# One core's diffusion backbone step: where the sums for the fast FFN product are formed, which first pairs leave the second 512 tokens out, and which engine does the norm's affine maps

## The chip, the cores and the metric

One core of a Trainium2 chip runs the whole inference step in one launch. The metric is device time in microseconds; the kernel before takes 3452.81 us, the median of 3 runs from 3447.42 to 3453.67. TensorE (PE) multiplies matrices out of SBUF into PSUM banks, VectorE (DVE), ScalarE (ACT) and GpSimd (POOL) do the elementwise work, and SyncE (SP) issues most DMAs; ScalarE and GpSimd issue some too. Each engine takes its instructions in the order in which they are written.

## The reference

Two layers, each a token mixer (S5 in layer 0, grouped-query attention in layer 1) and a SwiGLU FFN, on 1024 latent and 256 context tokens of width 1024. Cut to what the change touches:

```python
z = jax.nn.gelu(y)                               # S5 mixer
val, gate = jnp.split(z @ w_glu, 2, axis=-1)
ms = (val * jax.nn.sigmoid(gate)) @ w_out
xs = layer_norm(ALPHA * xs + g1 * ms, ln_g, ln_b)  # x for the residual
h = xs * (1.0 + sc2) + sh2                         # modulate
gate, up = jnp.split(h @ w_in, 2, axis=-1)         # FFN, w_in 1024 x 5632
fs = (jax.nn.silu(gate) * up) @ w_out              # 2816 x 1024
xs = layer_norm(ALPHA * xs + g2 * fs, ln_g, ln_b)
```

## The kernel before, in words

Activations lie transposed: 128 channels (a tile `kt` of 8) by tokens, in three chunks: c=0 and c=1 are 512 latent tokens each, c=2 the 256 context tokens. All matrix products run in float32 through a split: an operand x becomes hi = x rounded to TensorE's fast float32 form (ScalarE, a copy) and lo = x - hi (a subtract), and a product is hi*hi + hi*lo + lo*hi, three matmuls.

**The fast product.** `Ffn` computes the GLU of the S5 layer (8 pairs) and the first product of both FFNs (22 pairs each). A pair is 128 columns of gate and the 128 of up that belong to them. Over its latent tokens a pair is a product of 2x2 blocks (gate/up by chunk c=0/c=1 and by halves of the channels), done by a Strassen-Winograd scheme with 7 products instead of 8; each is 12 matmuls of 128x512 (L946). The weight side needs A11, A12, A21, A22 and the sums S1 to S4 (`i_step`), made anew for each pair. The token side needs B11, B21 (the two halves of c=0), B22 (second half of c=1) and the sums T1 to T4 of c=0 and c=1 (`x_next`: a subtract L848 on VectorE, hi L851 on ScalarE, lo L852 on VectorE or GpSimd by turns; 4 tiles each); they are made once per matrix. The context goes separately, as G and U, 24 matmuls of 128x256 each (L956). A whole pair is `FULL`: P1 P5 P6 P2 P7 G P4 P3 U.

P1 and P2 need only c=0 and G, U only the context. So the first pairs (`GF` = 2 in the GLU, `FF1` = 3 in each FFN) are cut in two: first all the `HEAD`s (P1, P2, G, U), before c=1 is ready, then the `TAIL`s (P6, P5, P7, Z3, P4). P1's product stays in its PSUM bank from head to tail, and the tail's P6, P7, P4 accumulate onto it; Z3 has a bank of its own. The first tail's steps call `x_all` for the sums they need (`ready` in `ffn_body`), so that T1, T2 are written ahead of P6, T3 ahead of P5, B22 ahead of P7, T4 ahead of Z3.

**The boundaries.** Between the output product of one sublayer and the first product of the next stands a layer norm over channels. `boundary` interleaves the output product, the norms' steps (a generator per chunk, `layer_norm`) and the heads, by an estimated clock and the estimated costs that each step yields. A norm of a chunk is: mean by a ones matmul (L695), subtract and square, the sum of squares (L711), rsqrt on VectorE (13 small instructions), its spread to all partitions (L691), then per tile a multiply (L718) and an affine map to h (even tiles on ScalarE L730, odd on VectorE L728). After these come 8 second affine maps in place to the residual (even on ScalarE L752, odd on GpSimd L748), each followed by a DMA of the tile to DRAM from the same engine's queue (`keep`, L1521). Last, h is split (`h_split`, hi L825, lo L826). Such boundaries stand before FFN 0, before the attention, before FFN 1, and, with no h, at the end.

Weights come by SyncE's DMAs, two raw half pages per pair; `AHEAD` = 4 operands are split ahead of their use. Pages (88 of 128x512) and half pages (13) are pools that wait for the last reader.

Of the kernel before, what the change touches and what calls it, by code (L numbers as in the profile page):

```python
# [613 lines left out]
class Dense(S5):  # L614
# [64 lines left out]
    def layer_norm(self, acc, c, cols, raw, ready, after=None):  # L679
# [36 lines left out]
        for kt in range(KT):  # L716
            a = acc[kt][c]
            v.tensor_tensor(a, a, pr, op=ALU.mult)  # L718
            if A is not None:
                if c < 2:  # L720
                    t = self.page()
                elif kt % 2 == 0:
                    pair = self.page(F32, (P, 2, 256))
                if c == 2:
                    t = pair[:, kt % 2, :]
                raw[kt][c] = t
                if kt % 2:
                    v.tensor_scalar(t, a, A[:, kt, cd:cd + 1], B[:, kt, cd:cd + 1], op0=ALU.mult, op1=ALU.add)  # L728
                else:
                    nc.scalar.activation(t, a, AF.Identity, bias=B[:, kt, cd:cd + 1], scale=A[:, kt, cd:cd + 1])  # L730
            else:
                self.affine(acc, cols, kt, c, after)
            if kt % 2:
                yield YW[5] * n / 512
        ready[c] = True
        if A is not None:
            for kt in range(KT):
                self.affine(acc, cols, kt, c, after)
                if kt % 2:
                    yield YW[6] * n / 512  # L740

    def affine(self, acc, cols, kt, c, after):
# [4 lines left out]
        if kt % 2 if cols[0] is not None else c == 2 and kt in (1, 3, 5):  # L747
# [8 lines left out]
    def boundary(self, outs, passes, ln, heads, ready):  # L756
# [41 lines left out]
        "P6": ("S2", "T2"), "P7": ("S3", "T3"), "Z3": ("S4", "B22")}  # L798
# [4 lines left out]
TAIL = ("S1", "S2", "S3", "S4", "A22"), ("P6", "P5", "P7", "Z3", "P4")  # L803

AHEAD = 4
# [4 lines left out]
class Ffn(Dense):  # L810
# [18 lines left out]
    def x_next(self, n):  # L829

        nc, r = self.nc, self.xr
        v, g = nc.vector, nc.gpsimd
# [4 lines left out]
        eng = (v, g)[k % 2]  # L837
        if n == "C":
            self.h_split(k, 2, eng)
        elif n[0] == "B":  # L840
            kt, c = k + 4 * (n[1] == "2"), int(n[2]) - 1
            self.h_split(kt, c, eng)
            self.X[n][k] = self.hs[kt, c]
        else:
# [7 lines left out]
            eng.tensor_tensor(lo, t, hi.bitcast(F32), op=ALU.subtract)  # L852
# [7 lines left out]


    def i_start(self, win, pairs, first):
# [3 lines left out]
        self.segs = [(t, HEAD) for t in p[:first]] + [(t, TAIL) for t in p[:first]] + [(t, FULL) for t in p[first:]]  # L866
# [4 lines left out]
    def i_load(self):  # L871
        if self.il < len(self.segs):
            r = []
            for h in range(2):
# [6 lines left out]
    def i_step(self):  # L881
# [6 lines left out]
        if a < n:  # L888
# [3 lines left out]
            g, u = self.iraw[i]  # L892
# [32 lines left out]
    def ffn_step(self, i, kind, act):  # L925
# [33 lines left out]
        if kind == "P1":  # L959
            R = product("R", True)  # L960
            e["s1"] = self.page()
            ac(e["s1"], R, AF.Copy)
        elif kind == "P2":
            B = product("B", True)
            v.tensor_tensor(e["s1"], e["s1"], B, op=ALU.add)  # L965
            ac(e["s1"], e["s1"], act)
        elif kind == "P5":
            product("Q", True)
        elif kind == "P6":
            R = product("R", False)  # L970
            e["s2"] = self.page()
            ac(e["s2"], R, AF.Copy)
        elif kind == "P7":
            R = product("R", False)
            x = e["t22"] = self.page()
            v.tensor_copy(x, e["Q"])
            v.tensor_tensor(x, x, R, op=ALU.add)
        elif kind == "P4":
            R = product("R", False)
            v.tensor_tensor(e["s1"], e["s1"], R, op=ALU.mult)  # L980
            self.spill(t, 0, e["s1"])
        elif kind in ("P3", "Z3"):
# [18 lines left out]
    def ffn_heads(self, act, first):  # L1001

        U = []
        for i in range(first):
            for kind in HEAD[1]:
                U.append((kind, lambda i=i, kind=kind: self.ffn_step(i, kind, act)))
        h0 = [lambda: self.x_all("B11", "B21")] + [u for k, u in U[:2]]
        h2 = [lambda: self.x_all("C")] + [u for k, u in U[2:]]
        return [(0, h0), (2, h2)]

    def ffn_body(self, act, first, last):
        ready = {0: ("T1", "T2"), 1: ("T3",), 2: ("B22",), 3: ("T4",)}
        for i in range(first, len(self.segs)):
# [462 lines left out]
NHP = 13, 88  # L1476

GF, FF1 = 2, 3


class Full(Attn):
# [31 lines left out]
    def rest(self):  # L1513
# [58 lines left out]
        self.ffn_body(AF.Sigmoid, GF, last)  # L1572
        acc = new()
# [5 lines left out]
        def ffn(l, cols, outs, acc, passes):  # L1579

            raw = self.xr
            self.cross(outs, TWO, acc, cols, raw, ready, self.ffn_heads(AF.Silu, FF1), keep)
# [431 lines left out]
```

## Time and profile before

| what | before |
|---|---|
| median of 3 runs | 3452.81 us |
| the profiled execution | 3445.47 us, its span 3443.4 us |
| mean granted TensorE clock | 0.957 |
| TensorE busy | 3200.7 us, 93% |
| VectorE busy | 2126.4 us, 62% |
| ScalarE busy | 1350.6 us, 39% |
| GpSimd busy | 402.4 us, 12% |
| L946 (the fast products) | 1053.7 us busy, 81.4 us idle before it |
| L956 (the context) | 323.2 us busy, 21.4 us idle before it |

Busy time is the sum of an engine's instructions in one execution; the idle time before a line is how long the engine stood still ahead of that line's instructions, with what ended it. The span starts at 0 for all times below. TensorE is busy almost throughout, so time is lost only where it waits or runs at a lower granted clock.

### The profile page before, as it was taken

The numbers are of one execution on the slowest core, as the hardware profiler recorded it, in microseconds if no ns is written. First come the engines' busy times: TensorE is split into PE (matmuls) and PEld (weight loads), VectorE is DVE, ScalarE is ACT, GpSimd is POOL, SyncE is SP. The second block draws the span as 40 slices with busy tenths as digits, with TensorE's granted clock in tenths as the row PEclk, the third lists the DMA queues.
The fourth block names the chain that finished last, engine by engine and source line by source line (L and its number), as shares of the span: only waits on it lengthen the run. The fifth ranks groups of instructions, "written<-read, shape, count | busy, mean of one in ns | idle before, by whom it ended". The sixth has DMA issues, their size and how long they took to land.

```text
span 3443.4 us, 46852 instructions
## 1 busy us (share of the span) xinstructions
PE 3200.7 (93%) x17674; PEld 2678.0 (78%) x17674; DVE 2126.4 (62%) x4317; ACT 1350.6 (39%) x2667; POOL 402.4 (12%) x420
## 2 busy tenths in 40 slices
PE   8999669997799999999989999999779999999997
PEld 5753647886588888887878899998558888888776
DVE  8789745557754444524676888885775444453645
ACT  3351432335422222412443577774442222232433
POOL 2230120013200000010232310001230000000001
PEclk9999779998899999999999999999879999999998
DMA  7679952243222221624421100102322121244544
GB/s 262 168 215 324 253 137 76 87 157 114 83 71 68 65 75 61 207 65 140 143 93 57 62 21 16 35 1 94 112 87 78 60 80 60 80 152 137 170 128 137
DMA packets 226563, 381.42 MB, mean 111 GB/s; under 512 B 54608, under 2 KB 109680, under 8 KB 225568
## 3 DMA queue, kind: packets, MB, share of 16 engines
q1 hardware_dynamic: 208000, 332.49, 30.7%
q0 software_dynamic: 10128, 33.22, 3.0%
q10 hardware_dynamic: 8208, 12.72, 1.0%
q8 instruction: 138, 2.26, 0.3%
q14 instruction: 89, 0.73, 0.1%
HBM read 297.61 MB, written 80.74 MB: 110 GB/s over the span
## 4 chain that ended last, share of the span: by engine, by line
PE 76%; DVE 12%; issue 4%; ACT 3%; DMA 3%; SPq 1%; POOL 1%; ACTq 0%; DVEq 0%; POOLq 0%
PE ps L946 27%; PE ps L123 9%; PE ps L121 9%; PE ps L125 9%; PE ps L956 8%; PE ps L1375 2%; DVE sw L537 1%; PE ps L1396 1%; PE ps L1395 1%; PE ps L1394 1%; PE ps L1333 1%; PE ps L1334 1%; PE ps L1335 1%; DVE X L543 1%; DVE sw L541 1%
## 5 line engine op out<-in xcount | busy, mean ns | idle before, releaser
L946 PE MATMUL ps<-pg,pg 128*128 128x512 f32 x4368 | 1053.7, 399 | 81.4 <-ACT pg L851 43.7
L946 PEld LDWEIGHTS ps<-pg,pg 128*128 128x128 f32 x4368 | 830.8, 193 | 273.6 <-ACT pg L851 50.9
L121 PE MATMUL ps<-pg,pg 128*128 128x512 f32 (+1 forms) x1872 | 639.7, 364 | 33.8 <-ACT pg L131 18.9
L123 PE MATMUL ps<-pg,pg 128*128 128x512 f32 (+1 forms) x1872 | 634.0, 361 | 5.7 <-DVE pg L132 3.7
L125 PE MATMUL ps<-pg,pg 128*128 128x512 f32 (+1 forms) x1872 | 629.1, 358 | 0.2 <-DVE pg L103 0.2
L121 PEld LDWEIGHTS ps<-pg,pg 128*128 128x128 f32 x1872 | 349.9, 191 | 98.6 <-ACT pg L131 23.3
L123 PEld LDWEIGHTS ps<-pg,pg 128*128 128x128 f32 x1872 | 349.7, 191 | 65.1 <-DVE pg L132 9.2
L125 PEld LDWEIGHTS ps<-pg,pg 128*128 128x128 f32 x1872 | 349.5, 191 | 52.8 <-DVE pg L103 1.3
L956 PE MATMUL ps<-pg,pg 128*128 128x256 f32 x2496 | 323.2, 287 | 21.4 <-ACT pg L825 21.4
L956 PEld LDWEIGHTS ps<-pg,pg 128*128 128x128 f32 x2496 | 319.6, 196 | 30.0 <-ACT pg L825 22.4
L102 ACT ACTIVATE pg<-wr 128x512 fp32r<-128x512 f32 x344 | 192.0, 597 | 362.7 <-DMA wr<-in_w_ffn_out 168.0
L103 DVE TENSOR_TENSOR pg<-wr,pg 128x512 fp32r<-128x512 f32 x344 | 261.2, 798 | 102.8 <-ACT pg L102 91.3
L631 DVE SCALAR_TENSOR_TENSOR pg<-ps,mods,pg 128x512 f32<-128x512 f32 x64 | 47.9, 749 | 275.4 <-PE ps L125 266.2
L910 DVE TENSOR_TENSOR pg<-pg,pg 128x512 fp32r<-128x512 f32 x208 | 143.0, 687 | 77.4 <-ACT pg L906 77.4
L1105 POOL TENSOR_TENSOR pg<-pg,pg 128x512 f32<-128x512 f32 x8 | 10.7, 1332 | 1523.4 <-DVE pg L631 968.6
L132 DVE TENSOR_TENSOR pg<-ps,pg 128x512 fp32r<-128x512 f32 (+1 forms) x210 | 141.8, 676 | 58.9 <-ACT pg L131 53.3
L910 DVE TENSOR_TENSOR pg<-wr,pg 128x512 fp32r<-128x512 f32 x216 | 154.5, 719 | 24.4 <-ACT pg L906 24.4
L1355 ACT ACTIVATE pg<-ps,nb,rq 128x512 f32<-128x512 f32 x192 | 148.8, 776 | 5.6 <-DVE sm L1364 2.6
L131 ACT ACTIVATE pg<-ps 128x512 fp32r<-128x512 f32 (+1 forms) x210 | 123.3, 588 | 67.8 <-PE ps L1375 47.6
L980 DVE TENSOR_TENSOR pg<-pg,ps 128x512 f32<-128x512 f32 x52 | 35.7, 687 | 178.1 <-PE ps L946 177.9
L965 DVE TENSOR_TENSOR pg<-pg,ps 128x512 f32<-128x512 f32 x52 | 35.7, 687 | 175.1 <-PE ps L946 174.4
L906 ACT ACTIVATE pg<-wr 128x512 fp32r<-128x512 f32 x216 | 132.1, 620 | 14.6 <-DMA wr<-in_w_s_glu 12.9
(341 smaller groups left out, 4738.1 us busy)
## 6 DMA issues: line engine op xcount, KB each, us to landing
wr<-in_w_ffn_in SPq DMA_DIRECT2D x100, 512.0 KB, 3.6
gw<-in_w_mod SPq DMA_DIRECT2D x192, 256.0 KB, 5.0
wr<-in_w_ffn_out SPq DMA_DIRECT2D x80, 512.0 KB, 3.8
dI<-pg SPq DMA_DIRECT2D x104, 256.0 KB, 4.6
pg<-dI SPq DMA_DIRECT2D x104, 256.0 KB, 4.9
wr<-in_w_ffn_out SPq DMA_DIRECT2D x40, 384.0 KB, 3.9
pg<-dX SPq DMA_DIRECT2D x48, 256.0 KB, 4.0
wr<-in_w_s_glu SPq DMA_DIRECT2D x20, 512.0 KB, 3.7
```

What stands on the lines that cost most here:

```text
L102: nc.scalar.activation(hi, x, AF.Copy)
L103: nc.vector.tensor_tensor(lo, x, hi.bitcast(F32), op=ALU.subtract)
L121: mm(ps[c], wh, rh[c], start=first, stop=False)
L123: mm(ps[c], wh, rl[c], start=False, stop=False)
L125: mm(ps[c], wl, rh[c], start=False, stop=last)
L131: self.nc.scalar.activation(hi, src, AF.Copy)
L132: self.nc.vector.tensor_tensor(lo, src, hi.bitcast(F32), op=ALU.subtract)
L906: nc.scalar.activation(hi, self.isum[i, name], AF.Copy)
L910: v.tensor_tensor(lo, self.isum[i, name], hi.bitcast(F32), op=ALU.subtract)
L946: mm(e[bank], p[:, o], q, start=(first and k == 0 and j == 0), stop=(k == 3 and j == 2), skip_group_check=True)
L956: mm(ps, p[:, o], q, start=(k == 0 and j == 0), stop=(k == KT - 1 and j == 2))
L1355: nc.scalar.activation(p, u["bank"].pop((qt, kc)), AF.Exp, bias=nb[:, 0:1], scale=rq, accum_out=sm[:, kc:kc + 1])
```

## The change

- `layer_norm`: all 8 affine maps to h on ScalarE; `affine`: all 8 second maps and their DMAs on ScalarE's queue (the final norm is as before).
- `x_next`: all lo subtracts on VectorE.
- `x_rest` yields T1, T2, T3, T4, B22 one tile at a time; the norm of c=1 takes two of them behind each of its 8 second affine maps, the rest behind the last. In the GLU two are taken behind each product from the third on.
- `GF` = (5, 0), `FF1` = (2, 3): 5 pairs are cut in two everywhere. The first 5 (GLU) or 2 (FFN) of them have `HEAD0` (P1, P2, one raw half page) and `TAIL0` (P6 P5 P7 G P4 P3 U), the other 3 of an FFN `HEAD` and `TAIL`.
- P1's product is copied to a page at once; in a tail P6 starts a fresh bank, VectorE adds the page to it (L992 of the changed kernel), P7 goes on in the same bank, and the page is added again for P7 and P4. P3 accumulates onto P5 and P7's bank, so Z3 is gone.
- `AHEAD` = 3 in heads and tails and 5 after; the norm's costs count 1.4 times (`YS`) in the FFN boundaries; 12 half pages; c=1 of the GLU's input is loaded before the context.

```diff
@@ layer_norm, affine
-                if kt % 2:
-                    v.tensor_scalar(t, a, A[:, kt, cd:cd + 1], B[:, kt, cd:cd + 1], op0=ALU.mult, op1=ALU.add)
-                else:
-                    nc.scalar.activation(t, a, AF.Identity, bias=B[:, kt, cd:cd + 1], scale=A[:, kt, cd:cd + 1])
+                nc.scalar.activation(t, a, AF.Identity, bias=B[:, kt, cd:cd + 1], scale=A[:, kt, cd:cd + 1])
...
         if A is not None:
+            then = iter(then)
             for kt in range(KT):
                 self.affine(acc, cols, kt, c, after)
-                if kt % 2:
-                    yield YW[6] * n / 512
+                t = next(then, 0.0) + next(then, 0.0)
+                if kt % 2 or t:
+                    yield t or YW[6] * n / 512
+            yield from then
...
-        if kt % 2 if cols[0] is not None else c == 2 and kt in (1, 3, 5):
+        if cols[0] is None and c == 2 and kt in (1, 3, 5):
@@ order of the first pairs
-TAIL = ("S1", "S2", "S3", "S4", "A22"), ("P6", "P5", "P7", "Z3", "P4")
-
-AHEAD = 4
+TAIL = ("S1", "S2", "S3", "A22", "S4"), ("P6", "P5", "P7", "P4", "P3")
+
+HEAD0 = ("A11", "A12"), ("P1", "P2")
+TAIL0 = ("S1", "S2", "S3", "A11", "A12", "A22", "S4", "A21"), ("P6", "P5", "P7", "G", "P4", "P3", "U")
+
+AHEAD = 3, 5
+
+YT, YS = 1.8, 1.4
@@ x_next
-            eng.tensor_tensor(lo, t, hi.bitcast(F32), op=ALU.subtract)
+            v.tensor_tensor(lo, t, hi.bitcast(F32), op=ALU.subtract)
...
+    def x_rest(self, *names):
+
+        for n in names or ("T1", "T2", "T3", "T4", "B22"):
+            while self.x_next(n):
+                yield YT
@@ ffn_step
+        self.x_all(*{"T2": ("T1", "T2"), "T4": ("T1", "T2", "T4")}.get(PROD.get(kind, (0, "C"))[1], (PROD.get(kind, (0, "C"))[1],)))
...
         elif kind == "P6":
-            R = product("R", False)
+
+            R = product("R", tail)
+            if tail:
+                e["p1"] = e["s2"]
             e["s2"] = self.page()
-            ac(e["s2"], R, AF.Copy)
+            if tail:
+                v.tensor_tensor(e["s2"], e["p1"], R, op=ALU.add)
+            else:
+                ac(e["s2"], R, AF.Copy)
         elif kind == "P7":
             R = product("R", False)
             x = e["t22"] = self.page()
-            v.tensor_copy(x, e["Q"])
+            if tail:
+                v.tensor_tensor(x, e["p1"], e["Q"], op=ALU.add)
+            else:
+                v.tensor_copy(x, e["Q"])
             v.tensor_tensor(x, x, R, op=ALU.add)
@@ constants and the GLU
-NHP = 13, 88
-
-GF, FF1 = 2, 3
+NHP = 12, 88
+
+GF, FF1 = (5, 0), (2, 3)
...
-        for c in (0, 2, 1):
+        for c in (0, 1, 2):
             zload(c)
-        heads = self.ffn_heads(AF.Sigmoid, GF)
-        for c, units in heads:
+        self.x_all("B11", "B21")
+        rest, k = self.x_rest("T1", "T2", "T3", "T4", "B22", "C"), 0
+        for c, units in self.ffn_heads(AF.Sigmoid):
             for u in units:
                 u()
+                k += 1
+                for _ in range(2 if k > 2 else 0):
+                    next(rest, None)
```

The first place is VectorE's queue at the first tail of the first FFN. Before: L848 and L852 are the sums' subtracts and splits, L826 splits of B22, L901 and L910 of the weights, L976 the first reading of the tail's banks.

```order
L848 TENSOR_TENSOR pg_1779_8352<-pg_1732_8204,pg_1726_8165 128x512
L852 TENSOR_TENSOR pg_1781_8355<-pg_1779_8352,pg_1780_8354 128x512
L848 TENSOR_TENSOR pg_1782_8358<-pg_1733_8207,pg_1727_8168 128x512
L826 TENSOR_TENSOR pg_1787_8378<-pg_1730_8198,pg_1786_8377 128x512
L826 TENSOR_TENSOR pg_1791_8386<-pg_1732_8204,pg_1790_8385 128x512
L901 TENSOR_TENSOR pg_1794_8393<-wr_1704_8056,pg_1764_8310 128x512
L910 TENSOR_TENSOR pg_1796_8397<-pg_1764_8310,pg_1770_8322 128x512
L976 COPY pg_1797_8411<-ps_1785_8364 128x512
L977 TENSOR_TENSOR pg_1797_8411<-pg_1797_8411,ps_1637_7728 128x512
L848 TENSOR_TENSOR pg_1798_8414<-pg_1591_7537,pg_1752_8286 128x512
L852 TENSOR_TENSOR pg_1800_8417<-pg_1798_8414,pg_1799_8416 128x512
```

The last four tiles (T4) stood behind the first tail's P7, here its L976 and L977. Of the changed kernel (L852 and L856 are the sums, L831 B22, L914 and L923 the weights, L992 the reading of P6's bank, which P7 goes on with):

```order
L852 TENSOR_TENSOR pg_1827_8474<-pg_1627_7661,pg_1803_8418 128x512
L856 TENSOR_TENSOR pg_1829_8477<-pg_1827_8474,pg_1828_8476 128x512
L831 TENSOR_TENSOR pg_1831_8481<-pg_1778_8357,pg_1830_8480 128x512
L831 TENSOR_TENSOR pg_1833_8485<-pg_1779_8360,pg_1832_8484 128x512
L831 TENSOR_TENSOR pg_1835_8489<-pg_1780_8363,pg_1834_8488 128x512
L831 TENSOR_TENSOR pg_1837_8493<-pg_1781_8366,pg_1836_8492 128x512
L923 TENSOR_TENSOR pg_1839_8498<-wr_1722_8070,pg_1770_8308 128x512
L914 TENSOR_TENSOR pg_1840_8500<-wr_1722_8070,pg_1747_8206 128x512
L923 TENSOR_TENSOR pg_1842_8504<-wr_1722_8070,pg_1838_8496 128x512
L992 TENSOR_TENSOR pg_1844_8519<-pg_1663_7778,ps_1843_8506 128x512
L923 TENSOR_TENSOR pg_1847_8536<-wr_1723_8072,pg_1841_8502 128x512
L999 TENSOR_TENSOR pg_1848_8550<-pg_1663_7778,ps_1845_8521 128x512
```

All sums and B22 now stand ahead of the first reading of a tail's bank.

The second place is ScalarE's queue behind the norm of c=1 that goes before the attention. Before: L752 are second affine maps, L1521 their DMAs, L1225 and L131 belong to a projection that runs beside it, L825 are the hi parts of h.

```order
L1225 ACTIVATE hp_3059_15737<-ps_3056_15707 128x256
L131 ACTIVATE pg_3058_15736<-ps_3056_15707 128x256
L752 ACTIVATE pg_2859_14671<-pg_2859_14671,ba_2480_12569,ga_2479_12568 128x512
L1521 DMA dX_73<-pg_2859_14671 128x512
L1225 ACTIVATE hp_3062_15772<-ps_3060_15746 128x256
L131 ACTIVATE pg_3061_15771<-ps_3060_15746 128x256
L752 ACTIVATE pg_2907_14944<-pg_2907_14944,ba_2480_12569,ga_2479_12568 128x512
L1521 DMA dX_73<-pg_2907_14944 128x512
L825 ACTIVATE pg_3063_15781<-pg_3037_15606 128x512
L825 ACTIVATE pg_3065_15785<-pg_3038_15609 128x512
```

Of the changed kernel (L1542 the DMAs, L1246 for L1225, L830 the hi parts):

```order
L752 ACTIVATE pg_2932_14905<-pg_2932_14905,ba_2522_12643,ga_2521_12642 128x512
L1542 DMA dX_73<-pg_2932_14905 128x512
L1246 ACTIVATE hp_3104_15846<-ps_3102_15820 128x256
L131 ACTIVATE pg_3103_15845<-ps_3102_15820 128x256
L752 ACTIVATE pg_2949_15018<-pg_2949_15018,ba_2522_12643,ga_2521_12642 128x512
L1542 DMA dX_73<-pg_2949_15018 128x512
L752 ACTIVATE pg_2966_15119<-pg_2966_15119,ba_2522_12643,ga_2521_12642 128x512
L1542 DMA dX_73<-pg_2966_15119 128x512
L830 ACTIVATE pg_3105_15855<-pg_3079_15680 128x512
L830 ACTIVATE pg_3107_15859<-pg_3080_15683 128x512
```

The hi parts stand behind 8 second affine maps and 8 DMAs where there were 4 of each; the other 4 were on GpSimd.

## Rows read from the trace of the kernel before

**Rows 1.** ScalarE's timeline, copies of first products, GLU, steady part (start, us, engine, line, ..., [idle before])
```profile
546.50 0.60 ACT L962 ACTIVATE pg<-ps 128x512 f32<-128x512 f32 x1 [3.10 <-PE ps L946]
...
571.34 0.60 ACT L962 ACTIVATE pg<-ps 128x512 f32<-128x512 f32 x1 [3.28 <-PE ps L946]
```

**Rows 2.** TensorE's timeline, start of the first FFN
```profile
812.70 0.73 PE L946 MATMUL ps<-pg,pg 128*128 128x512 f32 x2 [2.30 <-ACT pg L906]
818.55 4.64 PE L946 MATMUL ps<-pg,pg 128*128 128x512 f32 x10 [5.12 <-DVE pg L910]
822.98 1.02 PE L695 MATMUL ps<-hp,ones 128*128 128x256 f32 x2
...
842.46 8.48 PE L956 MATMUL ps<-pg,pg 128*128 128x256 f32 x48 [5.78 <-ACT pg L825]
...
857.14 5.92 PE L956 MATMUL ps<-pg,pg 128*128 128x256 f32 x48
...
872.01 2.05 PE L691 MATMUL ps<-ident,rstd 128*128 128x128 f32 x8 [2.35 <-DVE rstd L677]
...
893.30 0.79 PE L946 MATMUL ps<-pg,pg 128*128 128x512 f32 x1 [13.00 <-ACT pg L851]
...
923.61 36.65 PE L946 MATMUL ps<-pg,pg 128*128 128x512 f32 x155 [0.24 <-POOL pg L852]
```

**Rows 3.** ScalarE's timeline, first copy (L962) of a whole pair, first FFN
```profile
955.53 0.60 ACT L962 ACTIVATE pg<-ps 128x512 f32<-128x512 f32 x1 [3.04 <-PE ps L946]
```

**Rows 4.** TensorE's timeline, first tail of the second FFN
```profile
2545.36 0.80 PE L946 MATMUL ps<-pg,pg 128*128 128x512 f32 x1 [13.01 <-ACT pg L851]
```

**Rows 5.** Stretches, first FFN (us, then busy time of each engine, granted clock, DMA)
```profile
885.30:905.80 20.50, 10.85 (x22) 6.99 (x23) 14.78 (x20) 9.16 (x15) 6.00 (x5) 0.50 0.20 70
...
930.00:952.00 22.00, 22.00 (x99) 18.22 (x98) 12.90 (x21) 5.49 (x11) 0.00 (x0) 1.00 0.23 82
```

**Rows 6.** ScalarE's timeline, norm of the second 512 tokens, first FFN
```profile
880.22 0.81 ACT L730 ACTIVATE pg<-pg,B,A 128x512 f32<-128x512 f32 x1 [0.96 <-DVE pg L718]
...
884.43 0.81 ACT L752 ACTIVATE pg<-pg,ba,ga 128x512 f32<-128x512 f32 x1 [0.43 <-ACT pg L752]
...
885.65 0.81 ACT L752 ACTIVATE pg<-pg,ba,ga 128x512 f32<-128x512 f32 x1 [0.41 <-ACT pg L752]
```

**Rows 7.** VectorE's timeline, same stretch and the sums behind it
```profile
879.50 1.28 DVE L718 TENSOR_TENSOR pg<-pg,ps 128x512 f32<-128x512 f32 x2
...
888.13 1.29 DVE L848 TENSOR_TENSOR pg<-pg,pg 128x512 f32<-128x512 f32 x2
...
891.30 1.28 DVE L848 TENSOR_TENSOR pg<-pg,pg 128x512 f32<-128x512 f32 x2
...
915.58 0.69 DVE L848 TENSOR_TENSOR pg<-pg,pg 128x512 f32<-128x512 f32 x1
...
917.62 1.28 DVE L848 TENSOR_TENSOR pg<-pg,pg 128x512 f32<-128x512 f32 x2
```

**Rows 8.** VectorE's timeline, splits of the first 512 tokens
```profile
809.55 8.34 DVE L826 TENSOR_TENSOR pg<-pg,pg 128x512 fp32r<-128x512 f32 x3 [0.35 <-ACT pg L825]
```

**Rows 9.** GpSimd's timeline, the same splits
```profile
811.13 4.95 POOL L826 TENSOR_TENSOR pg<-pg,pg 128x512 fp32r<-128x512 f32 x4
```

**Rows 10.** TensorE's timeline, start of the GLU
```profile
452.11 1.22 PE L946 MATMUL ps<-pg,pg 128*128 128x512 f32 x2 [11.90 <-ACT pg L906]
...
498.01 0.79 PE L946 MATMUL ps<-pg,pg 128*128 128x512 f32 x1 [7.58 <-ACT pg L851]
```

**Rows 11.** VectorE's timeline, weights of the GLU
```profile
467.17 1.29 DVE L910 TENSOR_TENSOR pg<-wr,pg 128x512 fp32r<-128x512 f32 x2 [11.92 <-ACT pg L906]
```

**Rows 12.** TensorE's timeline, second 512 tokens ahead of attention
```profile
1799.11 0.49 PE L121 MATMUL ps<-pg,pg 128*128 128x512 f32 x1 [2.54 <-ACT pg L825]
...
1802.66 0.80 PE L123 MATMUL ps<-pg,pg 128*128 128x512 f32 x1 [1.35 <-POOL pg L826]
```

**Rows 13.** ScalarE's timeline, same place
```profile
1798.43 4.27 ACT L825 ACTIVATE pg<-pg 128x512 fp32r<-128x512 f32 x8 [0.40 <-ACT pg L752]
```

More of the change, by code (lines that the diff above doesn't have):

```diff
@@ L677, in rsqrt, with layer_norm @@
             v.scalar_tensor_tensor(out if it == 2 else y, t, 1.5, y, op0=ALU.add, op1=ALU.mult)
-    def layer_norm(self, acc, c, cols, raw, ready, after=None):
+    def layer_norm(self, acc, c, cols, raw, ready, after=None, then=()):
         nc = self.nc
@@ L754, in affine, with boundary @@
             after(nc.scalar, kt, c)
-    def boundary(self, outs, passes, ln, heads, ready):
+    def boundary(self, outs, passes, ln, heads, ready, slow=1.0):
         gens = []
@@ L766, in step @@
                 t = YW[0]
-            return t
+            return t * slow
         def run(units):
@@ L865, in i_start @@
         p = list(pairs)
-        self.segs = [(t, HEAD) for t in p[:first]] + [(t, TAIL) for t in p[:first]] + [(t, FULL) for t in p[first:]]
+        a, b = first[0], sum(first)
+        self.nhead = b
+        self.segs = [(t, HEAD0 if t < a else HEAD) for t in p[:b]] + [(t, TAIL0 if t < a else TAIL) for t in p[:b]] + \
+                    [(t, FULL) for t in p[b:]]
         self.items = [(i, n) for i, (_, (names, _)) in enumerate(self.segs) for n in names]
@@ L873, in i_load @@
             r = []
-            for h in range(2):
+            for h in range(1 if self.segs[self.il][1] is HEAD0 else 2):
                 x = self.w_raw()
@@ L930, in ffn_step @@
         e = self.ev.setdefault(t, {})
+        head, tail = (self.segs[i][1] in z for z in ((HEAD, HEAD0), (TAIL, TAIL0)))
+        self.x_all(*{"T2": ("T1", "T2"), "T4": ("T1", "T2", "T4")}.get(PROD.get(kind, (0, "C"))[1], (PROD.get(kind, (0, "C"))[1],)))
         ops = {"G": ("A11", "A12"), "U": ("A21", "A22")}.get(kind) or (PROD[kind][0],)
@@ L999, in ffn_step, with ffn_heads, ffn_body @@
         return 5.9 / 2 if kind in "GU" else 2.75
[L1001 to L1013, printed above, removed]
+    def ffn_heads(self, act):
+        U = [(kind, lambda i=i, kind=kind: self.ffn_step(i, kind, act))
+             for i in range(self.nhead) for kind in self.segs[i][1][1]]
+        k = next((k for k, (kind, _) in enumerate(U) if kind in "GU"), len(U))
+        return [(0, [u for _, u in U[:k]]), (2, [u for _, u in U[k:]])]
+    def ffn_body(self, act, last):
+        for i in range(self.nhead, len(self.segs)):
             for s, kind in enumerate(self.segs[i][1][1]):
-                if i == first:
-                    self.x_all(*ready.get(s, ()))
                 if i == len(self.segs) - 1:
@@ L1590, in ffn_hook @@
             self.i_start(L("w_ffn_in", l), range(NF), FF1)
-            return some(0, ("B11", "B21"), 8) + [lambda k=k: self.i_until(k) for k in range(4)] + some(2, ("C",), 8)
+            return some(0, ("B11", "B21"), 8) + [lambda k=k: self.i_until(k) for k in range(6)] + some(2, ("C",), 8)
         outs = lambda: self.out_chunks(acc, self.mod(0, 2), KT, TWO, inputs, ALPHA, ffn_hook(0))
```

43 lines of the change are left out of this document (23 added, 20 removed).

## The prediction

> **What bounds the kernel now.** I read the page's table of costly groups first: TensorE is busy 93% of the span, so time lies where it stands still or runs at the lower clock. Then its timeline at each place that the change touches, and the timelines of the engine it waits for.
>
> In the steady part nothing waits for the norm: two first products of whole pairs are 24.84 us apart [rows 1]. A G with its U takes some 5.9 of that (the row at 857.14) [rows 2], which leaves (24.84 - 5.9)/7 = 2.7 for a product. The change leaves whole pairs as they are, so the steady part keeps its time, and what counts is how long each start takes, up to the first whole pair.
>
> In the first FFN TensorE begins at 812.70, stands 5.12 us until VectorE has split the weights, then 5.78 at the context's first product, 2.35 at the norm's spread, and 13.00 at the first tail, which waits for the first sums [rows 2]. The first whole pair's first product is copied at 955.53 [rows 3]. The three pairs done by then are 3 x 24.84 = 74.5 us of work, in 955.53 - 2.7 - 812.70 = 140. The rest is waits and the lower clock: in the 20.5 us around the first tail the granted clock is 0.50, of the two levels the 1.2 GHz one, behind the wait of 13.00, and it is 1.00 later, where TensorE never stops [rows 5]. The second FFN has the same wait, 13.01 us [rows 4].
>
> **The change, part by part.** The profiled execution took 3445.5 us, the median of the runs is 3452.8; I count differences and add them to both.
>
> *FFN start, splits of c=0.* VectorE's three lo subtracts took 8.34 us in one row while GpSimd did its four in 4.95 [rows 8, 9]; without GpSimd one takes 0.69 [rows 7]. Eight on VectorE alone, each behind its hi of 0.53 (4.27 for 8) [rows 13], end 5 us after they start. Against that, ScalarE has four more second maps with their DMAs in front of them, 885.65 - 884.43 = 1.22 each [rows 6], some of them inside the longer spaced steps. The first product of pair 0 runs through from 816.4 instead of 818.55: 2 us won.
>
> *FFN heads.* Behind P1, P2 of pair 0 now come those of pair 1. So L695 for the context is not issued at 822.98 but after two pairs of products at partly half clock, at about 830 (816.4, four products of 2.7, and 2.6 for the lower clock: 10 matmuls took 4.64 in the row at 818.55). The chain from there to the context's first product took 842.46 - 822.98 = 19.5 [rows 2] and is set by norm steps on VectorE and ScalarE; with all affine maps on ScalarE I take 21, so the context starts at 851. Up to the spread L691 of c=1 lie two G,U and most of a third (8.48, 5.9, 5.9) and two pairs of products (2 x 5.4), 31 us, with some matmuls of the norm 33: 884, against 872.01. Of this lateness of 12 us the four extra products pay for 10.9.
>
> *Sums.* The spread is followed on VectorE by eight multiplies, 0.60 apart (two in 1.28, pipelined) [rows 7], from 886 to 891, and on ScalarE by eight affine maps of 0.81, some 0.7 apart as pipelined ones stand, where it had four [rows 6], and one second map with its DMA, until 894. Then the 16 tiles T1 to T4. On VectorE alone a tile's lo waits for the tile's hi; the row at 915.58 shows it, 2.04 us from one subtract to the next. Two tiles shared with GpSimd took 891.30 - 888.13 = 3.17, so the change makes two cost 4.1 [rows 7]. ScalarE's second map and DMA between them (1.22) and two hi (1.1) fit under that. Sixteen tiles end at about 927, the four B22 (0.7 each) and three instructions for weights at 930.5, and only then comes the reading of P6's bank, as the order of VectorE's queue shows. P6 itself starts with the first tile of T2, at 903, paced by the tiles to 911; P5 ends at 914. P7 accumulates into P6's bank, so it waits for that reading: TensorE stands still for 16 us, from 914 to 930.5. Before, T4 stood behind P7, so this wait did not exist. Then P7, G, P4, P3, U take 2.7 x 3 + 5.9 = 14, and some 3 for the lower clock that such waits brought [rows 5]: the first pair is done at 948. The other pair of the first sort needs 24.84 - 5.4 = 19.4, three tails 24.84 - 5.4 - 5.9 = 13.5 each: 1008. The first whole pair's copy falls at 1010.7, with two more pairs done; less 2 x 24.84 that is 961.0 against 955.53: **5.5 us lost, at each of two FFNs**. Bounds: if P7 were only held by T3 as before (about 919), 11 us less, a gain of 5.5; if the keep DMAs, all on one queue now, hold back pages that the sums want, 5 more.
>
> *The page for P1.* L992 takes the place of a copy on ScalarE, L999 that of a copy on VectorE; L1007 adds 0.69 per tail, 15 times. VectorE is busy 12.9 of 22 us in the tails [rows 5], so I take nothing; uncovered it would be 10 us in all.
>
> *GLU.* Ten products now come first, P1, P2 of five pairs, where there were two and a wait for the context. The second lot of weights is split at 467.17 as before [rows 11]. From the third product on VectorE does two tiles of sums behind each: 2 x 2.04, two lo of weights and an evacuation, 10 us for a pair against TensorE's 5.4. Four pairs end at about 508, P6 starts at 504 (498.01 before [rows 10]), P7 at 516, the first pair is done at 535 with the context's splits. Four more at 19.4 make 612.6, the copy 615.3, less 3 x 24.84: 540.8 against 546.50 [rows 1]: **5.7 us won**. Bounds: 0 to 12, by 5 either way in where the first pair ends.
>
> *Before the attention.* Here no head covers the norm of c=1. The hi row starts at 1798.43 and TensorE at 1799.11 [rows 12, 13]. Four more affine maps (0.7) and four more second maps with DMAs (1.22) stand in ScalarE's queue: up to 7.7 us. A map waited 0.96 for VectorE in the row at 880.22 [rows 6], and some of the added ones fill such waits, so I take 6.5 later. GpSimd, free of its own maps, gives the 1.35 back that the second tile waited for. **About 5 us lost**; bounds 2 and 7.7. The chunks c=0 and c=2 are ready there long before they are needed.
>
> The sum is 5.5 x 2 - 5.7 + 5 = 10.3, I take **+10**: 3455.5 for an execution like the profiled one, 3463 for the median.
>
> The Trainium skill's page "ScalarE: Activation LUTs" (Rules for kernel authors) says to leave multiplies and adds to VectorE. That speaks against the moved affine maps; here ScalarE's rows show 0.81 for one, and the terms above hold it already.
>
> **Rivals.**
>
> *The sums are covered: faster.* If VectorE reaches the reading of P6's bank by 919, because the tiles start during the norm's own steps or run faster than 2.04 without GpSimd, each FFN gains 5.5 instead: -11 - 5.7 + 5 = -12, 3441. For it: the 8.34 us of three subtracts beside GpSimd. Against it: in the round of 2.04 at 915.58 the two subtracts of 0.69 have no such excess; the other 0.7 is the way over ScalarE and back. The point is whether L992 issues before or after 919. By the Trainium skill's page "SBUF — State Buffer" (Who interferes with whom) a VectorE instruction with two inputs from SBUF contends with a GpSimd one that reads SBUF; the trace agrees (8.34 for three against 0.69), and by the rule each such overlap goes. I have it once per FFN, and it would not shorten a chain over ScalarE.
>
> *They cancel: no change.* With the GLU at its best (-12), the attention at +2 and the FFNs at +5 each the sum is 0: 3453.
>
> *Slower still.* The five pairs hold more pages (P1's products, sums, second maps waiting for one queue of DMAs), and the sums wait for them; with longer waits TensorE stays at 1.2 GHz for longer. 8 more per FFN, and 2.7 more at the attention: 10 + 16 + 3 = +29, 3482.
>
> **How the numbers follow.** Forecast +10, its own range +3 to +18 (3456 to 3471): 0.42. Faster by the first rival: 0.23. No change: 0.20. Slower still: 0.15. About 0.2%, 7 us, is what a measurement here can tell from nothing. What of the forecast's lower end would read as no change is in the 0.20. Faster 0.23, same 0.20, slower 0.57. The range, 3436 to 3482, leaves out the ends.
>
> **What would show it.** In the changed kernel's profile: TensorE idle for 10 to 20 us in front of the first P7 of each FFN, released by VectorE's L992, with L852 and L856 at 2.04 per tile right ahead of it; the first context product at about 851; the first whole pair's copy at about 1011 in the first FFN less what the GLU won, and at 615 in the GLU; L830 before the attention some 6 us later against its L727. Wrong would be L992 with no wait in front of P7, or a first whole pair that starts before 1000 less the GLU's gain.

## The result and the profile after

The changed kernel takes 3468.36 us, the median of 4 runs (3465.3 to 3475.9), against 3450.11 for the kernel before run beside it (4 runs, 3445.97 to 3453.67). The ratio is 1.0057, 95% interval 1.0035 to 1.0078: 19.7 us slower, give or take 7. The profiled execution took 3475.9 us and is the slowest of its four; its stages are compared below, not its end. The page, its table of engines and its costliest group:

```profile
span 3474.1 us, 46877 instructions
...
PE 3198.7 (92%) x17674; PEld 2675.3 (77%) x17674; DVE 2109.9 (61%) x4381; ACT 1401.9 (40%) x2740; POOL 274.5 (8%) x286
...
L961 PE MATMUL ps<-pg,pg 128*128 128x512 f32 x4368 | 1050.4, 399 | 121.3 <-ACT pg L919 61.7
```

TensorE is no busier; L961 (L946 of before) stands idle for 121.3 us ahead of its matmuls where it stood 81.4. The stages, read off TensorE's timelines of the two profiled executions:

| stage | before | after | difference |
|---|---|---|---|
| GLU, first fast product to the end of the last | 240.6 | 237.2 | -3.4 |
| first FFN, end of the output product ahead of it to its last product | 614.3 | 625.2 | +10.9 |
| norm ahead of attention, TensorE's waits for h | 4.1 | 7.4 | +3.3 |
| second FFN, as the first | 614.3 | 628.0 | +13.7 |

They sum to +24.5, in one execution each. The rest of the two executions differs by some 6 us more, most of it ahead of the GLU, whose first product comes at 457.36 instead of 452.11. Over the twelve kernels profiled here that time lies between 451 and 464 us without any order in it. Some 2 us lie around the attention, and what follows the second FFN is 1.4 shorter. From the first FFN's last L961 to the end of the output product ahead of the second FFN the changed kernel takes 1046.2 us, the kernel before 1040.9, so 5.3 more where the waits for h alone are 3.3.

TensorE's timeline at the start of the first FFN, which answers to [rows 2]:

```profile
817.50 1.22 PE L961 MATMUL ps<-pg,pg 128*128 128x512 f32 x2 [4.92 <-ACT pg L919]
...
852.12 8.26 PE L971 MATMUL ps<-pg,pg 128*128 128x256 f32 x48 [6.90 <-ACT pg L830]
...
886.55 1.16 PE L691 MATMUL ps<-ident,rstd 128*128 128x128 f32 x8 [1.23 <-DVE rstd L677]
904.15 12.15 PE L961 MATMUL ps<-pg,pg 128*128 128x512 f32 x24 [16.45 <-ACT pg L855]
931.91 4.63 PE L961 MATMUL ps<-pg,pg 128*128 128x512 f32 x12 [15.61 <-ACT pg L919]
...
947.60 8.35 PE L961 MATMUL ps<-pg,pg 128*128 128x512 f32 x36
...
967.00 5.63 PE L961 MATMUL ps<-pg,pg 128*128 128x512 f32 x24
974.71 2.98 PE L961 MATMUL ps<-pg,pg 128*128 128x512 f32 x12 [2.09 <-DVE pg L992]
978.57 11.17 PE L961 MATMUL ps<-pg,pg 128*128 128x512 f32 x48 [0.87 <-DVE pg L1002]
990.90 2.99 PE L961 MATMUL ps<-pg,pg 128*128 128x512 f32 x12 [1.16 <-DVE pg L992]
994.76 14.16 PE L961 MATMUL ps<-pg,pg 128*128 128x512 f32 x60 [0.87 <-DVE pg L1002]
1009.79 19.33 PE L961 MATMUL ps<-pg,pg 128*128 128x512 f32 x84 [0.87 <-DVE pg L1002]
1028.96 3.04 PE L971 MATMUL ps<-pg,pg 128*128 128x256 f32 x24
```

The output product ahead of this FFN ends at 812.58, 2.19 us later than before (810.39); that much of each time below is no part of the FFN. The first product runs through from 817.50 (before, it stood 5.12 us). The context starts at 852.12, the spread of the second 512 tokens' norm at 886.55, P6 at 904.15 behind a wait of 16.45. P7 starts at 931.91 behind 15.61, and the first pair ends at 947.60. The row of P7 puts its wait down to ScalarE's L919, but the operand it names was there long before, and VectorE's timeline shows what came last, the reading of P6's bank at 931.09:

```profile
896.17 0.69 DVE L856 TENSOR_TENSOR pg<-pg,pg 128x512 fp32r<-128x512 f32 x1 [2.77 <-ACT pg L855]
896.78 0.68 DVE L852 TENSOR_TENSOR pg<-pg,pg 128x512 f32<-128x512 f32 x1
898.16 0.69 DVE L856 TENSOR_TENSOR pg<-pg,pg 128x512 fp32r<-128x512 f32 x1 [0.69 <-ACT pg L855]
898.77 0.69 DVE L852 TENSOR_TENSOR pg<-pg,pg 128x512 f32<-128x512 f32 x1
...
926.87 2.49 DVE L831 TENSOR_TENSOR pg<-pg,pg 128x512 fp32r<-128x512 f32 x4
...
931.09 0.68 DVE L992 TENSOR_TENSOR pg<-pg,ps 128x512 f32<-128x512 f32 x1
```

From one lo subtract to the next (896.17 to 898.16) are 1.99 us, with VectorE idle for 0.7 in each round; all sixteen tiles and the four of B22 (926.87) come first, then L992. The clock in these stretches, as in [rows 5]:

```profile
895.00:905.00 10.00, 0.85 (x2) 0.41 (x2) 6.04 (x10) 4.67 (x8) 0.00 (x0) 0.50 0.21 79
905.00:915.40 10.40, 10.14 (x20) 5.75 (x21) 6.80 (x11) 5.26 (x8) 0.00 (x0) 0.52 0.14 50
930.00:940.00 10.00, 8.09 (x40) 7.05 (x41) 6.38 (x11) 2.33 (x5) 0.00 (x0) 0.73 0.23 67
```

It stands at 0.50 behind the wait for P6, so P6 and P5 take 12.15 us where 24 matmuls take 5.63 in the row at 967.00, and at 0.73 on the whole behind the wait for P7. The waits of 2.09, 0.87, 1.16, 0.87 and 0.87 in the later tails have no counterpart in before. The second FFN has the same two long waits:

```profile
2574.75 11.45 PE L961 MATMUL ps<-pg,pg 128*128 128x512 f32 x24 [16.47 <-ACT pg L855]
2602.52 5.46 PE L961 MATMUL ps<-pg,pg 128*128 128x512 f32 x12 [16.32 <-ACT pg L919]
```

The GLU, against [rows 10], and the copy that answers to [rows 1]:

```profile
457.36 7.40 PE L961 MATMUL ps<-pg,pg 128*128 128x512 f32 x24 [11.55 <-ACT pg L919]
...
509.69 8.06 PE L961 MATMUL ps<-pg,pg 128*128 128x512 f32 x22 [5.06 <-DVE pg L923]
521.58 4.58 PE L961 MATMUL ps<-pg,pg 128*128 128x512 f32 x12 [3.83 <-ACT pg L830]
...
542.24 8.35 PE L961 MATMUL ps<-pg,pg 128*128 128x512 f32 x36
```

```profile
622.78 0.60 ACT L977 ACTIVATE pg<-ps 128x512 f32<-128x512 f32 x1
```

In the GLU P6 starts at 509.69, P7 at 521.58, and the first pair ends at 542.24. Five pairs are done ahead of the copy at 622.78: 622.78 - 3 x 24.84 = 548.3 against 546.50, with a start 5.25 us later, so 3.4 us won. Ahead of attention, against [rows 12], one wait of 7.38 stands where there were 2.54, 0.23 and 1.35:

```profile
1818.49 0.79 PE L121 MATMUL ps<-pg,pg 128*128 128x512 f32 x1 [7.38 <-ACT pg L830]
```

### The profile page after: what moved, and what is told of

Same layout as the page of the kernel before. It is cut to its first block, busy times and chain, and to the rows that moved or that the text cites. A ratio compares the mean times of both kernels' runs of the same rounds, so it can differ in the third digit from the quotient of the medians.

```text
span 3474.1 us, 46877 instructions
## 1 busy us (share of the span) xinstructions
PE 3198.7 (92%) x17674; PEld 2675.3 (77%) x17674; DVE 2109.9 (61%) x4381; ACT 1401.9 (40%) x2740; POOL 274.5 (8%) x286
## 5 line engine op out<-in xcount | busy, mean ns | idle before, releaser
L961 PE MATMUL ps<-pg,pg 128*128 128x512 f32 x4368 | 1050.4, 399 | 121.3 <-ACT pg L919 61.7
L961 PEld LDWEIGHTS ps<-pg,pg 128*128 128x128 f32 x4368 | 830.2, 192 | 310.6 <-ACT pg L919 71.8
L923 DVE TENSOR_TENSOR pg<-wr,pg 128x512 fp32r<-128x512 f32 x232 | 158.1, 685 | 41.9 <-ACT pg L919 41.9
L919 ACT ACTIVATE pg<-pg 128x512 fp32r<-128x512 f32 x208 | 129.8, 625 | 119.3 <-DVE pg L914 110.7
L1126 POOL TENSOR_TENSOR pg<-pg,pg 128x512 f32<-128x512 f32 x8 | 10.6, 1330 | 1863.4 <-DVE pg L631 1119.7
L131 ACT ACTIVATE pg<-ps 128x512 fp32r<-128x512 f32 (+1 forms) x210 | 123.8, 591 | 65.9 <-PE ps L1396 47.6
L919 ACT ACTIVATE pg<-wr 128x512 fp32r<-128x512 f32 x232 | 137.6, 620 | 28.2 <-DMA wr<-in_w_s_glu 14.7
L923 DVE TENSOR_TENSOR pg<-pg,pg 128x512 fp32r<-128x512 f32 x208 | 142.3, 685 | 0.2
L1015 ACT ACTIVATE pg<-pg 128x512 f32<-128x512 f32 x52 | 32.9, 632 | 262.6 <-DVE pg L1014 262.6
```

What stands on the lines that cost most here:

```text
L131: self.nc.scalar.activation(hi, src, AF.Copy)
L919: nc.scalar.activation(hi, self.isum[i, name], AF.Copy)
L923: v.tensor_tensor(lo, self.isum[i, name], hi.bitcast(F32), op=ALU.subtract)
L961: mm(e[bank], p[:, o], q, start=(first and k == 0 and j == 0), stop=(k == 3 and j == 2), skip_group_check=True)
```

## The experiments

All times are medians; ratios are to the kernel before, run beside each. The working theory was the prediction's: in an FFN all twenty tiles stand in VectorE's queue ahead of L992, for which P7 waits; ScalarE's queue costs some microseconds ahead of attention.

**Sums when the first tail needs them.**

```diff
-            ... self.ffn_heads(AF.Silu), keep, self.x_rest())
+            ... self.ffn_heads(AF.Silu), keep, iter(()))
```

> The changed kernel, but in the two FFNs the sums T1 to T4 and B22 are not taken inside the norm; each is written when the first tail needs it (T1, T2 ahead of P6, T3 behind the reading of P6's bank L992, T4 ahead of P4, B22 ahead of P3). Theory (P7 waits for L992, which stands behind all twenty tiles in VectorE's queue): L992 issues some 18 us earlier, P7 is then paced by T3 and P4 by T4, the first pair of the first sort ends 5 to 8 us earlier than the changed kernel's 947.6; 11 to 16 us less in all than the changed kernel. Rival (the sum of VectorE's work for the twenty tiles sets the end, wherever they stand): no change, within 3 us. The wait of 16.5 us in front of P6 stays by both.

3487.76 us, ratio 1.0105 (1.0091 to 1.0119): 17 us slower than the changed kernel, where 11 to 16 faster was expected. Both expectations fail. TensorE ahead of P6, and ScalarE ahead of the first sum's hi part:

```profile
910.29 4.89 PE L961 MATMUL ps<-pg,pg 128*128 128x512 f32 x7 [24.97 <-ACT pg L855]
```

```profile
891.93 0.80 ACT L752 ACTIVATE pg<-pg,ba,ga 128x512 f32<-128x512 f32 x1
...
900.44 0.81 ACT L752 ACTIVATE pg<-pg,ba,ga 128x512 f32<-128x512 f32 x1 [0.41 <-ACT pg L752]
...
901.66 0.63 ACT L855 ACTIVATE pg<-pg 128x512 fp32r<-128x512 f32 x1 [0.40 <-ACT pg L752]
```

P6 waits 24.97 us instead of 16.45: without the sums between them, all eight second maps and their DMAs (891.93 to 901.66) stand ahead of the first hi. The edit moves L992 as well: P7 now follows P6 and P5 with no wait over 0.6 us. Counted from the FFN's first product, P6 starts 8.4 us later and the first pair ends 5.1 later, so being rid of the wait for L992, with T4 and B22 behind it, gave back 3.3. The prediction's bound for P7 held by T3 alone was 11. So the place of the sums inside the norm gains some 17 us against this kernel; it is not the loss.

**Affine maps on the engines of before.**

```diff
-                nc.scalar.activation(t, a, AF.Identity, ...)
+                if kt % 2:
+                    v.tensor_scalar(t, a, A..., B..., op0=ALU.mult, op1=ALU.add)
+                else:
+                    nc.scalar.activation(t, a, AF.Identity, ...)
...
-        if cols[0] is None and c == 2 and kt in (1, 3, 5):
+        if kt % 2 if cols[0] is not None else c == 2 and kt in (1, 3, 5):
```

> The changed kernel with the affine maps where they were before: odd tiles' maps to h on VectorE, odd tiles' second maps and their DMAs on GpSimd. Theory (ScalarE's queue delays the hi parts ahead of attention and the first sums): the stage before attention is 3 to 5 us shorter, each FFN's first sum 2 to 3 us earlier; 7 to 11 us less in all. Rival (the maps are covered, what counts is the place of the sums alone): within 3 us of the changed kernel.

3466.13 us, ratio 1.0047 (1.0034 to 1.006), some 3 us under the changed kernel, with overlapping intervals: nearer to the rival. Ahead of attention TensorE's waits are those of before again, 2.50 and 1.22 with 0.22 between:

```profile
1815.49 0.50 PE L121 MATMUL ps<-pg,pg 128*128 128x512 f32 x1 [2.50 <-ACT pg L833]
...
1819.05 0.79 PE L123 MATMUL ps<-pg,pg 128*128 128x512 f32 x1 [1.22 <-POOL pg L834]
```

The longer stretch around the attention is back at 1041.1 us. In the first FFN nothing moves (625.2 us), in the second 1 us. So of the attention term 3.4 us are the wait on ScalarE's queue, and in the FFNs the maps are covered. "ScalarE: Activation LUTs" (Rules for kernel authors) of the Trainium skill would leave such maps to VectorE; the direction agrees, the size is at the edge of what can be told, and the edit moves other maps to GpSimd at the same time.

**Every second lo subtract on GpSimd.**

```diff
-            v.tensor_tensor(lo, t, hi.bitcast(F32), op=ALU.subtract)
+            (v, nc.gpsimd)[k % 2].tensor_tensor(lo, t, hi.bitcast(F32), op=ALU.subtract)
```

> The changed kernel with every second lo subtract of the sums T1 to T4 on GpSimd again (B11, B21, B22 and the context stay on VectorE). Theory (the tiles' pace on VectorE sets L992): two tiles take 3.2 instead of 4.1 us, L992 comes 7 us earlier in each FFN, P6's bank is read earlier by as much, in the GLU the heads are 3 us shorter; 12 to 18 us less in all. Rival (contention of GpSimd with VectorE eats it): VectorE's subtracts take over 1.2 us beside GpSimd and two tiles stay at 4; within 4 us of the changed kernel.

3462.35 us, ratio 1.0036 (1.0023 to 1.0048): 7 us under the changed kernel, half of what was expected, with overlapping intervals. By stages 5.7 of it are in the GLU; the FFNs are 1.2 and 1.6 us shorter, and L992 comes 1.2 us earlier against the spread of the norm, not 7. VectorE's timeline over one round of two tiles, and ScalarE's in it:

```profile
886.75 1.29 DVE L852 TENSOR_TENSOR pg<-pg,pg 128x512 f32<-128x512 f32 x2
889.86 0.69 DVE L856 TENSOR_TENSOR pg<-pg,pg 128x512 fp32r<-128x512 f32 x1 [1.83 <-ACT pg L855]
890.47 1.28 DVE L852 TENSOR_TENSOR pg<-pg,pg 128x512 f32<-128x512 f32 x2
```

```profile
887.47 0.63 ACT L855 ACTIVATE pg<-pg 128x512 fp32r<-128x512 f32 x1 [1.36 <-DVE pg L852]
888.00 0.80 ACT L752 ACTIVATE pg<-pg,ba,ga 128x512 f32<-128x512 f32 x1
...
889.20 0.63 ACT L855 ACTIVATE pg<-pg 128x512 fp32r<-128x512 f32 x1 [0.40 <-ACT pg L752]
```

Two tiles take 3.72 us, not 3.2: the second map and its DMA (888.00 to 889.20) now stand in front of a hi part that VectorE waits for. VectorE's instructions keep their 0.69 and GpSimd's subtract falls into its wait, so contention, the rival's reason, is not what eats it.

**Three pairs cut in two in the FFNs.**

```diff
-GF, FF1 = (5, 0), (2, 3)
+GF, FF1 = (5, 0), (0, 3)
```

> The changed kernel with FF1 = (0, 3): the two pairs of the first sort are gone from the FFNs, three pairs are cut in two as before the change. Theory (the extra four products stand in front of the norm of the second 512 tokens and only put off the sums): the spread L691 of that norm comes 11 us earlier, L992 too, while 10.9 us of work go from in front of it to behind; 0 to 7 us less per kernel pair of FFNs than the changed kernel. Rival (the extra products fill waits and are a gain in themselves): 10 to 20 us more than the changed kernel.

3482.33 us, ratio 1.0085 (1.0072 to 1.0099), 10 us more than the changed kernel: the rival's side, though the two intervals just touch (1.0078 is the changed kernel's upper end). TensorE at the context's norm and at P7 of the first tail:

```profile
834.87 1.01 PE L711 MATMUL ps<-ones,hp 128*128 128x1 f32 x4 [8.94 <-DVE hp L706]
...
926.68 3.75 PE L961 MATMUL ps<-pg,pg 128*128 128x512 f32 x8 [16.65 <-DVE pg L992]
```

The wait at the sum of squares is 8.94 instead of 3.17, and the spread of the norm comes 5.5 us earlier against the FFN's start (880.23 against 886.55, the start 816.69 against 817.50), not 11. So half of the four extra products fills a wait, which the prediction took as a mere exchange.

**Each sum's lo behind the next sum's subtract.**

```diff
             nc.scalar.activation(hi, t, AF.Copy)
-            v.tensor_tensor(lo, t, hi.bitcast(F32), op=ALU.subtract)
+            self.x_lo()            # the lo of the tile before
+            self.xl = t, hi, lo
```

> The changed kernel with one edit: each sum's lo subtract is written behind the next sum's subtract, so that VectorE does not stand for 0.7 us on ScalarE's hi of the same tile. Theory (in the FFNs the way over ScalarE and back, 2.04 us a tile, sets when L992 and with it P7 comes): a tile takes 1.2 us, L992 in the first FFN comes at about 919 instead of 931, the wait in front of P7 shrinks from 15.6 to some 10; with the GLU's heads 3 to 8 us shorter, 22 to 35 us less in all than the changed kernel, under the kernel before. Rival (VectorE's own work or the lower clock sets the stage): less than 8 us.

3440.48 us, ratio 0.9969 (0.9953 to 0.9984): 30 us under the changed kernel and 11 under before. VectorE's timeline, with L864 the lo and L1002 the reading of P6's bank:

```profile
896.06 0.68 DVE L852 TENSOR_TENSOR pg<-pg,pg 128x512 f32<-128x512 f32 x1
...
897.27 0.68 DVE L852 TENSOR_TENSOR pg<-pg,pg 128x512 f32<-128x512 f32 x1
...
916.49 0.68 DVE L1002 TENSOR_TENSOR pg<-pg,ps 128x512 f32<-128x512 f32 x1
```

A tile takes 1.21 us. From the spread of the norm to the reading of P6's bank pass 33.1 us (883.42 to 916.49) instead of 44.5; the wait ahead of P7 is 11.46, P6 starts 3 us earlier against the spread. By stages: GLU -12.4, the FFNs -11.4 and -12.2. The way over ScalarE and back set the pace, as the prediction had it.

**P3 ahead of P4 in the later tails.**

```diff
-TAIL = ("S1", "S2", "S3", "A22", "S4"), ("P6", "P5", "P7", "P4", "P3")
+TAIL = ("S1", "S2", "S3", "S4", "A22"), ("P6", "P5", "P7", "P3", "P4")
```

> The changed kernel with P3 ahead of P4 in the tails of the second sort. Theory (P4 accumulates onto the bank that VectorE's L1002 is still reading behind P7, 0.87 us in each of three tails of each FFN, a term that the prediction costed at nothing): the 0.87 waits go, 5 us less in all. Rival (the tails are bound by weights or VectorE anyway): the wait moves to P3 or to the next P6, within 1 us.

The weights S4 and A22 change places with the products that use them. 3455.93 us, ratio 1.0014 (1.0003 to 1.0025): 15 us under the changed kernel, three times the expectation, and 5 above the kernel before. TensorE, from the first of the three tails to the first whole pair's context:

```profile
962.28 54.59 PE L961 MATMUL ps<-pg,pg 128*128 128x512 f32 x240
1016.70 3.04 PE L971 MATMUL ps<-pg,pg 128*128 128x256 f32 x24
```

All five waits are gone, the two for L992 too: the three tails and five products, 240 matmuls, run in one piece and take 54.4 us where they took 1028.96 - 967.00 = 62.0. That is 7.6 us for an FFN, 5.9 of it the waits named above; the rest, and the 9.0 of the second FFN, I have not split further.

**A bank of its own for P7 in the tails.**

```diff
-            R = product("R", False)
+            R = product("R", tail)
...
-                v.tensor_tensor(x, e["p1"], e["Q"], op=ALU.add)
+                v.tensor_tensor(x, e["s2"], e["Q"], op=ALU.add)
...
-                v.tensor_tensor(x, x, R, op=ALU.add)
+                v.tensor_tensor(x, e["s2"], R, op=ALU.add)
```

> The changed kernel with a fresh PSUM bank for P7 in the tails (t22 and P4 then add the page of P1 + P6). Theory (P7 waits only because it goes on in the bank that L992 has to read): P7 starts with T3, some 14 us earlier in each FFN, and the waits of 2.0 and 1.1 ahead of the later P7s go; but P4 still waits for L1002 behind all sums in VectorE's queue, so the first pair ends only 3 to 6 us earlier; 8 to 16 us less in all. Rival (the sums' end sets it whatever the bank): P7 early, the first pair's end where it was, less than 4 us.

3454.42 us, ratio 1.0013 (1.0003 to 1.0023): 15 us under the changed kernel, within the expectation. TensorE from P6 on:

```profile
900.20 14.61 PE L961 MATMUL ps<-pg,pg 128*128 128x512 f32 x34 [16.45 <-ACT pg L855]
...
926.07 5.06 PE L971 MATMUL ps<-pg,pg 128*128 128x256 f32 x22 [10.06 <-DVE pg L923]
```

P7 follows P6 and P5 with no long wait (34 matmuls in the first row), which shows that the bank is what held it. 10.06 us of the wait turn up behind it, at G, whose weights are split behind the sums on VectorE. By stages the FFNs are 7.6 and 10.6 us shorter, the first pair of the first FFN 4.4 of it.

**The kernel before, with overlapped sums**: the edit of "Each sum's lo behind the next sum's subtract", with all lo subtracts of the sums on VectorE. Here every second one of them leaves GpSimd as well, and this run does not separate the two.

> The kernel before with the sums' lo subtracts all on VectorE and each behind the next sum's subtract. Theory (the pace of the sums sets the first tails of the kernel before too: 3.17 us for two tiles, and waits of 0.5 to 3.1 in front of the products): two tiles take 2.4, the first whole pair of an FFN starts 2 to 4 us earlier, 4 to 10 us less in all than before. Rival (weights and the lower clock set it): within 3 us of before.

3420.66 us, ratio 0.9917 (0.9898 to 0.9937): 29 us under before, three times the upper end of what was expected. The stretch from 885 to 960 us in before and in this kernel (PE busy first, the granted clock third from the end):

```profile
885.00:960.00 75.00, 60.00 (x213) 44.46 (x214) 52.98 (x74) 27.06 (x47) 13.85 (x10) 0.80 0.22 77
```

```profile
885.00:960.00 75.00, 58.40 (x237) 44.21 (x236) 58.67 (x92) 32.72 (x55) 7.42 (x8) 0.91 0.28 93
```

In an FFN the waits in front of the tails shrink by some 3 us, as expected (the first from 13.00 to 11.57, the small ones from 6.5 to 4.7 in all); what was left out is the clock, 0.91 instead of 0.80 over the stretch. The FFN starts 6 us later in this execution, so here are the same 240 matmuls of the two: from the first tail's P6 to the first whole pair's G (893.30 to 966.2 before, 898.30 to 964.2 here) TensorE is busy 66.20 and 60.87 us, at granted clocks of 0.84 and 0.95. No run changes the clock without the waits, so that the shorter waits raised it is argued. By stages: GLU -8.1, FFNs -7.9 and -8.4.

**Three edits in the changed kernel**: overlapped sums, P3 ahead of P4, affine maps as before.

> The changed kernel with three edits together: the lo subtracts behind the next sum's subtract, P3 ahead of P4 in the tails, the affine maps on the engines of before. Theory (the pace of the sums, the bank that VectorE still reads, and ScalarE's queue ahead of attention are three separate losses): the gains add, 38 to 44 us less than the changed kernel, 3424 to 3430. Rival (they are one loss, seen at three places): about what the first edit gives alone, 3440.

3414.32 us, ratio 0.9895 (0.9877 to 0.9913): 56 us under the changed kernel by the ratios. Alone the three gave 30, 15 and 3, so the gains add, with 8 us over that the intervals hardly tell; the losses were separate.

**The kernel before, with overlapped sums and all splits of h for the fast product on VectorE.**

```diff
-        eng = (v, g)[k % 2]
+        eng = v
```

> The kernel before with the sums' lo subtracts on VectorE behind the next sum's subtract, and the lo subtracts of B11, B21, B22 and the context on VectorE too. Theory (GpSimd's subtracts hold VectorE up: three took 8.34 us beside it, and TensorE stands 5.1 us in front of an FFN's first products): that wait goes to under 1 us, 4 to 10 us less than with the sums alone, 3410 to 3417. Rival (it is hidden by the norms' chain behind it): within 3 us of the kernel with the sums alone, 3421.

3409.8 us, ratio 0.9889 (0.9869 to 0.9908), 11 us under the kernel with the overlapped sums. VectorE's eight subtracts ahead of the first FFN, against [rows 8], and the wait they leave in front of the first products, against [rows 2]:

```profile
801.78 5.89 DVE L826 TENSOR_TENSOR pg<-pg,pg 128x512 fp32r<-128x512 f32 x8 [2.13 <-ACT pg L825]
```

```profile
808.33 4.21 PE L955 MATMUL ps<-pg,pg 128*128 128x512 f32 x9 [1.63 <-DVE pg L919]
```

Eight take 5.89 us where three took 8.34 beside GpSimd's four, and 5.12 of waiting become 1.63. It is the fastest kernel of all here, with the one above within its interval. "SBUF — State Buffer" (Who interferes with whom) of the Trainium skill says what the rows show: two inputs from SBUF on VectorE and a GpSimd instruction that reads SBUF get in each other's way.

## Why the prediction was right

*Direction and size.* Forecast +10 with a range from 3436 to 3482; measured 3468.36, +18 to +20. The sum was short by nearly half, and one term, put at nothing, is most of what it lacked.

*FFN, up to the first pair.* Forecast and measured: context 851 and 852.12; spread 884 and 886.55; P6 at 903 and 904.15; L992 at 930.5 and 931.09; P7 at 930.5 and 931.91; the first pair's end 948 and 947.6. Without the 2.19 us by which the changed kernel's FFN begins later, the last is 945.4, 2.6 us better than forecast. All as worked out, 2.04 us a tile included (1.99 measured), and the experiments with the overlapped sums and with P7's own bank show both links: the pace and the bank.

*The three tails behind it, the step that failed.* The prediction let them run through, "three tails 24.84 - 5.4 - 5.9 = 13.5 each", and said of the page for P1: "VectorE is busy 12.9 of 22 us in the tails, so I take nothing." By its terms three tails and the five products behind them take 54.0 us. They took 62.0, and 54.4 with P3 ahead of P4. An average share hid the question of what is late, and two hand-overs were. The page for P1 put L992 on VectorE in place of a copy on ScalarE, and there it stands behind weights that come late:

```profile
971.47 0.69 DVE L914 TENSOR_TENSOR pg<-wr 128x512 f32<-128x512 f32 x1 [3.53 <-DMA wr<-in_w_ffn_in]
...
973.88 0.68 DVE L992 TENSOR_TENSOR pg<-pg,ps 128x512 f32<-128x512 f32 x1
```

P7 waits 2.09 and 1.16 us for it. P4's 0.87 in each tail is not the page's: the change's `TAIL` has P4 right behind P7, in the bank that L1002 reads, where Z3 stood between the two before. The prediction has no term for that. With P3 ahead of P4 the FFNs were 7.6 and 9.0 us shorter. Put in, the forecast of 5.5 becomes 5.5 + 8.0 - 2.6 = 10.9, against 10.9 and 13.7 measured; the uncovered cost that I gave for the page, 10 us in all, was the better term.

*What was luck.* Without these waits the changed kernel is 5 us above before (ratio 1.0014), less than the 7 us that the prediction could tell from nothing. That the change measured clearly slower is owed in the main to the term that was put at nothing.

*GLU.* Forecast 5.7 won, measured 3.4. The first pair ends at 542.2 - 5.25 = 537, not 535.

*Attention.* Forecast about 5 lost; 3.3 in the waits, 5.3 over the longer stretch, and both are back with the maps moved back.

*What the prediction did not see.* It laid the loss to the place of the sums ahead of L992. Taking them out of the norm cost another 17 us, and taking the extra heads out 10: two of the parts pay for themselves. The chain without overlap on VectorE is a cost of both kernels and not what sets them apart: with the sums overlapped in each, the changed one takes 3440.48 us and the one before 3420.66, ratios of 0.9969 and 0.9917, still 18 us. What takes the difference away is P3 ahead of P4 (15 us) and the maps moved back (3): with these and overlapped sums the changed kernel stands at 0.9895, level with the 0.9917 of the kernel before with overlapped sums, within the intervals. And the prediction priced the lower clock by a flat 3 us a place, where in the kernel before with overlapped sums 3 us less of waits went with 5 us less of matmul time at a higher clock (7.9 us gained in the first FFN).

## What to carry to other kernels

Where an engine hands a tile to a second one and takes it back, put the next tile's first step between: that was worth 30 us on the changed kernel, and 29 on the kernel before together with a move of subtracts from GpSimd to VectorE, more than any other single edit here. Before a product goes on in a PSUM bank that another engine reads, put an independent product between them, or give it a bank of its own. Price what is late at each hand-over, not the busy share of the engine that does it.

## What the hardware showed unexpectedly

Granted clock: small gaps between groups of matmuls at the first tails went with a clock of 0.80 over 75 us, and with some of them closed it was 0.91; 3.2 us less of waits at the first tail came with 7.9 us less for the FFN. The S5 mixer ahead of the GLU, which no kernel here changes, ended its last matmul between 438.8 and 452.2 us from one profiled execution to the next, a spread wider than many of the effects; stages were safer to compare than ends.
